# The low parts of 61 weight tiles: one subtraction on VectorE, or a copy on ScalarE and an accumulating DMA, in one layer of a hybrid backbone

## The chip, the cores and the metric

The kernel runs on one core of a Trainium2 chip. The metric is the device time of one execution in microseconds (us), lower is better; the profile gives beside it the span, which leaves out a little at both ends. The engines are PE (TensorE, matmuls; its weight loads are shown apart as PEld), DVE (VectorE), ACT (ScalarE), POOL (GpSimd) and SP (SyncE, which issues almost all DMAs). Each engine runs its instructions in a fixed order and waits on semaphores.

## The reference

One layer over 512 latent tokens and 256 context tokens of width 1024. What matters here is which weights are multiplied with what:

```python
h = rms_norm(x, g_norm1) * (1.0 + sc1) + sh1            # sc1, sh1, ... = silu(c) @ w_ada + b_ada
hc = rms_norm(ctx, g_norm1) * (1.0 + csc1) + csh1
aq, ak, av, dq, dk, dv, dz, da, db, ga, gd = split_cols(h @ w_in)
...
y_attn = window_ctx_attention(q_a, k_a, v_a, k_ac, v_ac, attn_sink)
o_dc, s_cf, s_cb = bidir_delta(...)                     # context scan, its states go on
o_dl, _, _ = bidir_delta(..., s_cf, s_cb)               # latent scan, chunks of 64
...
```

Each of the two mixers' results is projected to width 1024, weighted by a sigmoid gate, the two are summed and projected by `w_out`; a gated residual, a second norm and an MLP with squared ReLU (1024 to 4096 to 1024) follow.

## The kernel before, in words

**Split matmuls.** Nearly all matmuls run on fp32r operands, and to keep fp32 accuracy each operand is split into a high part (the value rounded to fp32r) and a low part (the value less its high part). A product is then three matmuls: high by high, high by low, low by high (`mm3`, L270, L271, L272; in the gate tiles and the branch projections the same three stand in L940 and L985). A weight tile holds 128 output columns and all rows of the contraction: 128x1024 numbers (512 KB), or 128x512 (256 KB) for a branch projection.

**Loading a weight tile** is `wload` (L254 to L263). SP starts the DMA of the raw tile into a slot of the ring `wr` (L256), which has NWR = 4 slots; ACT writes the high part `wh` (L261); DVE subtracts it from the raw tile and writes the low part `wl` (L262). The pairs `wh`, `wl` have NWS = 2 slots each. The list `wq` (L351 to L355) holds the tiles in the order in which PE takes them: 20 of `w_in` (the last three of DeltaNet's keys, attention's keys, queries and values, DeltaNet's values and queries, three gates), 8 of the first branch projection, 17 gates of `w_in`, 8 of the second branch projection, 8 of the output projection, 61 in all. `wnext` (L358) hands out the next one and starts to load the one behind it, so that one tile is ahead of the one in use. Two early tiles (L316) and the 64 tiles of the MLP (L1309, L1344, L1365) go through `wload` too, but into buffers of their own. The ring `wr` also takes the 32 tiles `wa` of the conditioning weights that are needed late; DVE multiplies them with the condition and sums along the row (`late_mod`, L1005, run in groups by `run_late` while the scan goes on, and the last eight beside the first quarter of the MLP).

**The stages**, by the span of the profile before:
- 0 to 66 us: norm and modulation of the inputs (`modulate`, L275 on DVE, L276 on ACT, L277 on DVE), with the two early tiles multiplied as each of the eight row blocks is ready.
- 66 to 320: key, query and value tiles; the attention and the inversion of the chunks' triangular matrices (a long sequence of small DVE operations, L770 and L771) are woven between them. Queries and keys pass a rotary embedding (`rope`: L405 is a multiplication on POOL, L404, L406 and L407 are on DVE).
- 320 to 520: the scan over chunks (`chain_step`), small dependent matmuls and DVE operations, with the branch projection of attention and the gate tiles as filler on PE.
- 520 to 606: the remaining gates, then the branch projection of DeltaNet (eight tiles of 12 matmuls of 512 columns), the output projection (eight tiles of 24), and the second norm.
- 606 to 957: the MLP, in quarters: eight tiles of the first matrix, eight of the second.

The order on each engine is fixed when the kernel is built: the code is woven by hand (`weave`), and a scheduler orders the instructions by their dependencies and the slots of the rings.

Of the kernel before, what the change touches and what calls it, by code (L numbers as in the profile page):

```python
# [11 lines left out]
AF = mybir.ActivationFunctionType  # L12
ALU = mybir.AluOpType
# [1 line left out]
PSUM = bass.MemoryType.PSUM  # L15

NU = 167
NWR, NWS = 4, 2
FILL = 144, 28, 36, (8, 7, 3)
INV = 2, 12, 18, 0  # L20
QTS = 7, 5, 4, 7, 3, 6, 10, 7
# [14 lines left out]
KT = D // P  # L36
# [60 lines left out]
def tile_layer(ctx: ExitStack, tc: tile.TileContext, I: dict, out: bass.AP, dbg=None):  # L97
    nc = tc.nc
    V, A, G, PE = nc.vector, nc.scalar, nc.gpsimd, nc.tensor
# [8 lines left out]
    def nm(s):  # L108
        uid[0] += 1
        return f"{s}_{uid[0]}"  # L110
# [19 lines left out]
    r32 = lambda ap: ap.bitcast(F32R)  # L130
# [120 lines left out]
        b.free()  # L251


    def wload(src, n=KT, bufs=None):  # L254
        raw = sb.tile([P, KT, P], F32, tag="wr", bufs=NWR, name=nm("wr"))[:, :n]
        nc.sync.dma_start(out=raw, in_=src)  # L256
        if bufs:
            hi, lo = (b.ap.rearrange("p (k c) -> p k c", k=KT) for b in bufs)
        else:
            hi, lo = (sb.tile([P, KT, P], F32, tag=t, bufs=NWS, name=nm(t))[:, :n] for t in ("wh", "wl"))  # L260
        A.activation(r32(hi), raw, AF.Copy)  # L261
        V.tensor_tensor(r32(lo), raw, hi, op=ALU.subtract)  # L262
        return r32(hi), r32(lo)  # L263

    def mm3(acc, w, xs, start=True, stop=True, ks=None):
# [20 lines left out]
    for kt in range(KT):  # L286
# [26 lines left out]
        if kt in EARLY:  # L313
            bb = alloc(1024), alloc(1024)
            ebufs += bb
            early.append((wload(I["win"][EARLY[kt]], bufs=bb), bank(2)))  # L316
# [28 lines left out]
    for n in range(2):  # L345
# [5 lines left out]
    wq = [(I["win"][t], KT) for t in (T_DK + 1, T_DK + 2, T_DK + 3, T_AK, *range(T_AQ, T_AQ + 4), T_AV, *range(T_DV, T_DV + 4),  # L351
                                      *range(T_DQ, T_DQ + 4), *(t + i for t, i in gates[:ND1]))]
    wq += [(I["wbr"][0, ct], 4) for ct in range(8)] + [(I["win"][t + i], KT) for t, i in gates[ND1:]]
    wq += [(I["wbr"][1, ct], 4) for ct in range(8)] + [(I["wout"][ct], KT) for ct in range(8)]
    wq = [lambda a=a: wload(*a) for a in wq]  # L355
    wn = [wq.pop(0)()]

    def wnext():  # L358
        w = wn.pop()
        if wq:  # L360
            wn.append(wq.pop(0)())
        return w

    def in_tile_steps(ti, with_ctx):

        for (_, e), t in zip(early, EARLY.values()):
            if t == ti:
                return e
        w = wnext()
        acc = bank(2 if with_ctx else 1)  # L370
        for k in range(KT):
            mm3(acc[:, :512], w, hx[k:k + 1], start=(k == 0), stop=(k == KT - 1), ks=[k])
            if with_ctx:
                mm3(acc[:, 512:768], w, hc[k:k + 1], start=(k == 0), stop=(k == KT - 1), ks=[k])
            if k < KT - 1:
                yield
        return acc
# [555 lines left out]
    def gate_tiles(todo):  # L933

        for kind, i in todo:
            w = wnext()
            acc = bank()
            for k in range(KT):
                for p, (x, y) in enumerate(((0, 0), (0, 1), (1, 0))):
                    PE.matmul(acc.ap, w[x][:, k, :], hx[k][y], start=(k == p == 0), stop=(k == KT - 1 and p == 2))  # L940
                    yield
            if kind == T_GA:
                g = alloc(SEQ)
                act(g.ap, acc.ap, AF.Tanh, scale=0.5)
                V.scalar_tensor_tensor(gat[i].ap, g.ap, 1.0, gat[i].ap, op0=ALU.add, op1=ALU.mult)
                g.free()
            else:
                t = alloc(SEQ, True)
                if kind == T_GD:
                    act(t.ap, acc.ap, AF.Tanh, scale=0.5)  # L950
                else:
                    silu2(t.ap, acc.ap)
                (gdt if kind == T_GD else szt).append(t)
            acc.free()
# [22 lines left out]
    def br_a():  # L977

        for ct in range(8):
            gat.append(alloc(SEQ, True))  # L980
            w = wnext()
            pa = bank()
            for j in range(4):
                for p, (x, y) in enumerate(((0, 0), (0, 1), (1, 0))):
                    PE.matmul(pa.ap, w[x][:, j, :], r32(Q[y][:, :, j, :]), start=(j == p == 0), stop=(j == 3 and p == 2))  # L985
                    yield
            A.activation(gat[ct].ap, pa.ap, AF.Copy)
            pa.free()
        for b in Qb:
            b.free()  # L990
# [8 lines left out]
    def late_mod(grp):  # L999

        for j in range(8):
            wa = sb.tile([P, KT, P], F32, tag="wr", bufs=NWR, name=nm("wa")).rearrange("p k c -> p (k c)")
            nc.sync.dma_start(out=wa, in_=I["wada2"][grp, j])
            t = alloc(1024)
            V.scalar_tensor_tensor(t.ap, wa, 0.5, scr.ap, op0=ALU.mult, op1=ALU.mult, accum_out=modT[:, grp, j:j + 1])  # L1005
            t.free()
            if j == 7:
                V.tensor_tensor(modT[:, grp], modT[:, grp], bada[:, 16 + 8 * grp:24 + 8 * grp], op=ALU.add)
            yield

    late = (x for grp in range(4) for x in late_mod(grp))
# [155 lines left out]
    for g in range(2):  # L1167
# [12 lines left out]
        for a in range(2):  # L1180
            lo, hi = quad(a, 0), quad(a, 1)
# [37 lines left out]
    for qq in range(2):  # L1219
# [3 lines left out]
        for a in range(2):  # L1223
            n = 2 * qq + a
# [16 lines left out]
    for ct in range(8):  # L1241
        w = wnext()
# [32 lines left out]
    for ct in range(8 - NHALF):  # L1275
        w = wnext()
# [29 lines left out]
    def load_first():  # L1306
        for i in range(NHALF):
            bufs = [alloc(1024), alloc(1024)]
            first.append([bufs, wload(I["wm1"][i], bufs=bufs)])  # L1309
# [27 lines left out]
    for hf in range(4):  # L1337
        act_ = []
        for f in range(FT):
            if first:  # L1340
                bufs, _, acc = first.pop(0)
            else:
                bufs = [alloc(1024), alloc(1024)]
                w = wload(I["wm1"][hf * FT + f], bufs=bufs)  # L1344
# [17 lines left out]
        for ct in range(8):  # L1362
            acc = bank()
            bufs = [alloc(1024), alloc(1024)]
            w = wload(I["wm2"][ct * 4 + hf], bufs=bufs)  # L1365
# [120 lines left out]
```

## Time and profile before

| | us |
|---|---|
| time, median of 3 runs (lowest to highest) | 960.3 (957.15 to 960.33) |
| the profiled execution | 959.2 |
| its span | 957.4 |
| PE busy | 917.7 |
| DVE busy | 597.9 |
| ACT busy | 449.3 |
| POOL busy | 36.4 |

The profiled execution is 1.8 us longer than its span, and 1.1 us under the median. In the views, L12 is line 12 of the kernel before; "out<-in" are the tiles that an instruction writes and reads; "<-" behind an idle time names what ended it ("issue": nothing that the profile shows). Matmuls are pipelined, so that one may count as busy while the next has begun.

### The profile page before, as it was taken

What the parts mean: (1) busy time and instruction counts of PE and PEld (TensorE: products, weight loads), DVE (VectorE), ACT (ScalarE), POOL (GpSimd) and SP (SyncE); (2) the same over time, 40 slices, a digit from 0 to 9 for tenths busy, and PEclk for the clock granted to TensorE, in tenths of its full rate; (3) what the DMA queues carried; (4) which work ended last, traced back from release to release, by engine and by line L of the source; (5) the groups of instructions that cost most, each with busy time, mean ns of one, the idle gap of its engine ahead of it and who ended that gap; (6) DMA issues with size and microseconds to landing.
All of it is one profiled execution on the core that took longest, in us unless ns stands there. A gap on an engine that the chain in (4) does not pass through costs nothing. (4 is left out here: it accounts for less than half of the span.)

```text
span 957.4 us, 18072 instructions
## 1 busy us (share of the span) xinstructions
PE 917.7 (96%) x7684; PEld 737.1 (77%) x7684; DVE 597.9 (62%) x1010; ACT 449.3 (47%) x827; POOL 36.4 (4%) x45
## 2 busy tenths in 40 slices
PE   7999989989999999869999999999999999999998
PEld 3578767876877677658887889988888888888886
DVE  0876688997788899745567665982365225423511
ACT  6456745337667887337555433561154115313400
POOL 0000221000000000100011000000000000000000
PEclk9999999999999999888999999999999999999999
DMA  9742012110000133850114544382164214322101
GB/s 354 250 167 67 23 47 66 48 64 24 12 21 25 38 107 111 295 192 25 46 61 129 185 134 154 119 272 72 35 212 134 82 66 130 113 66 71 62 33 55
DMA packets 29889, 99.77 MB, mean 104 GB/s; under 512 B 3696, under 2 KB 4208, under 8 KB 29808
## 3 DMA queue, kind: packets, MB, share of 16 engines
q1 hardware_dynamic: 29808, 98.62, 31.4%
q8 instruction: 60, 0.98, 0.4%
q14 instruction: 21, 0.17, 0.1%
HBM read 96.51 MB, written 2.10 MB: 103 GB/s over the span
## 5 line engine op out<-in xcount | busy, mean ns | idle before, releaser
L271 PE MATMUL banks<-m,m 128*128 128x512 f32 (+1 forms) x568 | 213.4, 378 | 0.0
L272 PE MATMUL banks<-m,m 128*128 128x512 f32 (+1 forms) x568 | 212.5, 377 | 0.0
L270 PE MATMUL banks<-m,m 128*128 128x512 f32 (+1 forms) x568 | 210.5, 379 | 1.7 <-ACT m L276 1.7
L261 ACT ACTIVATE m<-wr 128x1024 fp32r<-128x1024 f32 x66 | 69.9, 1059 | 150.3 <-PE banks L271 78.1
L270 PEld LDWEIGHTS banks<-m,m 128*128 128x128 f32 x568 | 105.5, 188 | 23.7 <-issue 1.9
L271 PEld LDWEIGHTS banks<-m,m 128*128 128x128 f32 x568 | 106.3, 188 | 21.3 <-DVE m L198 0.9
L272 PEld LDWEIGHTS banks<-m,m 128*128 128x128 f32 x568 | 106.4, 188 | 19.9
L262 DVE TENSOR_TENSOR m<-wr,m 128x1024 fp32r<-128x1024 f32 x66 | 80.6, 1224 | 63.9 <-PE banks L271 34.2
L270 PE MATMUL banks<-m,wh 128*128 128x512 f32 (+1 forms) x328 | 119.7, 365 | 0.0
L271 PE MATMUL banks<-m,wh 128*128 128x512 f32 (+1 forms) x328 | 116.4, 355 | 0.0
L272 PE MATMUL banks<-m,wl 128*128 128x512 f32 (+1 forms) x328 | 116.1, 355 | 0.1
L940 PE MATMUL banks<-m,wh 128*128 128x512 f32 x320 | 108.1, 413 | 0.0
L1367 DVE SCALAR_TENSOR_TENSOR m<-banks,modT,m 128x512 f32<-128x512 f32 x32 | 24.0, 750 | 104.0 <-PE banks L272 104.0
L261 ACT ACTIVATE wh<-wr 128x1024 fp32r<-128x1024 f32 (+1 forms) x61 | 57.7, 946 | 54.2 <-PE banks L940 24.4
L262 DVE TENSOR_TENSOR wl<-wr,wh 128x1024 fp32r<-128x1024 f32 (+1 forms) x61 | 65.8, 1079 | 20.8 <-ACT wh L261 20.7
L940 PEld LDWEIGHTS banks<-m,wh 128*128 128x128 f32 x320 | 62.1, 197 | 17.1 <-issue 4.1
L940 PE MATMUL banks<-m,wl 128*128 128x512 f32 x160 | 66.9, 418 | 4.3 <-issue 4.3
L272 PEld LDWEIGHTS banks<-m,wl 128*128 128x128 f32 x328 | 61.8, 189 | 9.3 <-DVE wl L262 0.6
L270 PEld LDWEIGHTS banks<-m,wh 128*128 128x128 f32 x328 | 61.9, 189 | 8.9 <-ACT m L276 0.4
L271 PEld LDWEIGHTS banks<-m,wh 128*128 128x128 f32 x328 | 62.0, 189 | 8.4 <-issue 0.5
L181 ACT ACTIVATE m<-m 128x512 fp32r<-128x512 f32 (+1 forms) x56 | 35.0, 630 | 47.4 <-DVE m L1350 19.8
L182 DVE TENSOR_TENSOR m<-m,m 128x512 fp32r<-128x512 f32 (+1 forms) x56 | 38.2, 689 | 20.9 <-ACT m L181 20.4
(232 smaller groups left out, 1325.8 us busy)
## 6 DMA issues: line engine op xcount, KB each, us to landing
wr<-in_wm SPq DMA_DIRECT2D x64, 512.0 KB, 3.5
wr<-in_win SPq DMA_DIRECT2D x39, 512.0 KB, 3.6
wa<-in_wada SPq DMA_DIRECT2D x32, 512.0 KB, 4.3
m<-in_wada SPq DMA_DIRECT2D x16, 512.0 KB, 10.1
m<-in_xT SPq DMA_DIRECT2D x8, 512.0 KB, 6.7
wr<-in_wbr SPq DMA_DIRECT2D x16, 256.0 KB, 2.7
wr<-in_wout SPq DMA_DIRECT2D x8, 512.0 KB, 3.6
out<-m SPq DMA_DIRECT2D x8, 256.0 KB, 2.0
```

Source lines behind the costliest of these rows:

```text
L181: A.activation(r32(hi), src, AF.Copy)
L182: (eng or V).tensor_tensor(r32(lo), src, hi, op=ALU.subtract)
L261: A.activation(r32(hi), raw, AF.Copy)
L262: V.tensor_tensor(r32(lo), raw, hi, op=ALU.subtract)
L270: PE.matmul(acc, w[0][:, k, :], xhi, start=(start and i == 0), stop=False)
L271: PE.matmul(acc, w[0][:, k, :], xlo, start=False, stop=False)
L272: PE.matmul(acc, w[1][:, k, :], xhi, start=False, stop=(stop and i == n - 1))
L940: PE.matmul(acc.ap, w[x][:, k, :], hx[k][y], start=(k == p == 0), stop=(k == KT - 1 and p == 2))
L1367: V.scalar_tensor_tensor(xn_[ct], acc.ap, modT[:, 3, ct:ct + 1], xn_[ct], op0=ALU.mult, op1=ALU.add)
```

## The change

For the 61 tiles of `wq`, DVE's subtraction is replaced by two steps: ACT writes the negative high part into the low part's buffer (it rounds the raw tile a second time, with a scale of -1), and a DMA that GpSimd issues reads the same weights from memory once more and adds them to what stands there. The early tiles and the MLP keep the subtraction. The ring of raw tiles has two slots and no longer four, the pairs have three and no longer two, and `wnext` keeps two tiles ahead.

```diff
-NWR, NWS = 4, 2
+NWR, NWS = 2, 3
+WAHEAD = 2
...
-    def wload(src, n=KT, bufs=None):
+    def wload(src, n=KT, bufs=None, late=False):
...
         A.activation(r32(hi), raw, AF.Copy)
-        V.tensor_tensor(r32(lo), raw, hi, op=ALU.subtract)
+        if late:
+            A.activation(r32(lo), raw, AF.Copy, scale=-1.0)
+            G.dma_start(out=r32(lo), in_=src, accum_op=ALU.add)
+        else:
+            V.tensor_tensor(r32(lo), raw, hi, op=ALU.subtract)
...
-    wq = [lambda a=a: wload(*a) for a in wq]
-    wn = [wq.pop(0)()]
+    wq = [lambda a=a: wload(*a, late=True) for a in wq]
+    wn = [wq.pop(0)() for _ in range(WAHEAD)]
...
-        w = wn.pop()
+        w = wn.pop(0)
```

In the changed kernel the lines behind the diff's first part move: the raw load is L258, the high part L263, ACT's negative part L265, the DMA L266, the subtraction L268, and what stood from L270 on stands six lines lower (L276 to L278 are `mm3`'s three matmuls).

On each engine 61 instructions move: DVE has 61 fewer, ACT 61 more, POOL issues 61 DMAs where it issued none. Each copies the whole tile: 45 of 512 KB and 16 of 256 KB, 27.3 MB of further reads of memory.

The first place is PE at the end of the input stage. `wh` and `wl` are the first tile of `wq`, numbers such as m_152 and m_153 are the modulated latent and context tokens, the other names are the two early tiles. Before, in the midst of the last row block:

```order
L271 MATMUL banks<-m_152,m_237 128x512
L272 MATMUL banks<-m_152,m_238 128x512
L271 MATMUL banks<-m_153,m_237 128x256
L272 MATMUL banks<-m_153,m_238 128x256
L272 MATMUL banks<-m_152,wl_469 128x512 [waits DVE_49]
L272 MATMUL banks<-m_153,wl_469 128x256
L270 MATMUL banks<-m_152,wh_468 128x512
L271 MATMUL banks<-m_152,wh_468 128x512
L272 MATMUL banks<-m_152,wl_469 128x512
L270 MATMUL banks<-m_153,wh_468 128x256
L271 MATMUL banks<-m_153,wh_468 128x256
L272 MATMUL banks<-m_153,wl_469 128x256
```

In the changed kernel, at the same row block:

```order
L277 MATMUL banks<-m_152,m_169 128x512 [waits DVE_49]
L278 MATMUL banks<-m_152,m_170 128x512
L277 MATMUL banks<-m_153,m_169 128x256 [waits DVE_49]
L278 MATMUL banks<-m_153,m_170 128x256
L277 MATMUL banks<-m_152,m_237 128x512
L278 MATMUL banks<-m_152,m_238 128x512
L277 MATMUL banks<-m_153,m_237 128x256
L278 MATMUL banks<-m_153,m_238 128x256
L278 MATMUL banks<-m_152,wl_469 128x512 [waits DMASW0_49]
L278 MATMUL banks<-m_153,wl_469 128x256
L276 MATMUL banks<-m_152,wh_468 128x512
L277 MATMUL banks<-m_152,wh_468 128x512
```

The matmuls with the first `wl`, which stood between the groups of the two early tiles, stand behind all of these groups, and the first of them waits for a DMA of POOL's queue (DMASW; DMAHW are SP's) in place of DVE.

The second place is ACT in the branch projection of DeltaNet: a high part for a coming tile alternates with the high part of a finished gated sum (`split`, L181 before). Before:

```order
L261 ACTIVATE wh_5877<-wr_5875 128x512 [waits DMAHW6_49,PE_49,Activation_49]
L181 ACTIVATE m_5824<-m_2935 128x512 [waits DVE_49]
L261 ACTIVATE wh_5899<-wr_5897 128x512 [waits DMAHW7_49,PE_49,Activation_49]
L181 ACTIVATE m_5825<-m_2967 128x512 [waits DVE_49]
L261 ACTIVATE wh_5921<-wr_5919 128x512 [waits DMAHW1_49,PE_49,Activation_49]
L181 ACTIVATE m_5826<-m_5599 128x512 [waits DVE_49]
```

In the changed kernel:

```order
L263 ACTIVATE wh_5932<-wr_5930 128x512 [waits DMAHW0_49,PE_49,Activation_49]
L265 ACTIVATE wl_5933<-wr_5930 128x512 [waits DMASW6_49,PE_49]
L182 ACTIVATE m_5877<-m_2962 128x512 [waits DVE_49]
L263 ACTIVATE wh_5955<-wr_5953 128x512 [waits DMAHW2_49,PE_49,Activation_49]
L265 ACTIVATE wl_5956<-wr_5953 128x512 [waits DMASW7_49,PE_49]
L182 ACTIVATE m_5878<-m_2995 128x512 [waits DVE_49]
L263 ACTIVATE wh_5978<-wr_5976 128x512 [waits DMAHW4_49,PE_49,Activation_49]
L265 ACTIVATE wl_5979<-wr_5976 128x512 [waits DMASW0_49,PE_49]
L182 ACTIVATE m_5879<-m_5648 128x512 [waits DVE_49]
```

Each high part is followed by the negative part of the same tile, and the finished sum's part stands behind both. In both kernels the high part waits for PE, which must be through with the slot's last tile.

The third place is POOL between 100 and 170 us of the span, where it computes parts of the chunks' matrices (L711) and the rotary embedding (L405). Before:

```order
L711 TENSOR_TENSOR m_1411<-c_nmask,btok 128x512 [waits DVE_49,Activation_49]
L405 TENSOR_TENSOR m_1055<-m_1055,m_454 128x512 [waits DVE_49,Activation_49,Pool_49]
L711 TENSOR_TENSOR m_1429<-c_nmask,btok 128x512 [waits PE_49]
L405 TENSOR_TENSOR m_1255<-m_1255,m_454 128x512 [waits DMAHW4_49,DVE_49,Activation_49]
L405 TENSOR_TENSOR m_1455<-m_1455,m_454 128x512 [waits DVE_49,Activation_49,Pool_49]
L405 TENSOR_TENSOR m_1524<-m_1524,m_454 128x512 [waits DVE_49,Activation_49]
```

In the changed kernel:

```order
L717 TENSOR_TENSOR m_1426<-c_nmask,btok 128x512 [waits DVE_49,Activation_49]
L266 DMA wl_1214<-in_win 128x1024 [waits DMASW4_49,PE_49,Activation_49]
L411 TENSOR_TENSOR m_1068<-m_1068,m_454 128x512 [waits DVE_49,Pool_49]
L717 TENSOR_TENSOR m_1444<-c_nmask,btok 128x512 [waits PE_49]
L266 DMA wl_1415<-in_win 128x1024 [waits DMASW5_49,PE_49,Activation_49]
L411 TENSOR_TENSOR m_1269<-m_1269,m_454 128x512 [waits DMAHW4_49,DVE_49]
L266 DMA wl_1500<-in_win 128x1024 [waits DMASW6_49,PE_49,Activation_49]
L411 TENSOR_TENSOR m_1470<-m_1470,m_454 128x512 [waits DVE_49,Pool_49]
L266 DMA wl_1558<-in_win 128x1024 [waits DMASW7_49,Activation_49]
L411 TENSOR_TENSOR m_1540<-m_1540,m_454 128x512 [waits DVE_49,Activation_49]
```

The DMAs stand between these operations, and each waits for ACT's negative part and for an earlier DMA of the queue, most of them for PE too; what stands behind one on POOL waits with it.

## The prediction

> **What bounds the kernel now.** I read the page's busy times first, and with them its list of DMA issues (KB each, median us from issue to landing), which the new work will be measured by.
>
> ```profile
> PE 917.7 (96%) x7684; PEld 737.1 (77%) x7684; DVE 597.9 (62%) x1010; ACT 449.3 (47%) x827; POOL 36.4 (4%) x45
> ...
> wr<-in_win SPq DMA_DIRECT2D x39, 512.0 KB, 3.6
> wa<-in_wada SPq DMA_DIRECT2D x32, 512.0 KB, 4.3
> ...
> wr<-in_wbr SPq DMA_DIRECT2D x16, 256.0 KB, 2.7
> wr<-in_wout SPq DMA_DIRECT2D x8, 512.0 KB, 3.6
> ```
>
> PE is busy for 96% of the span. Taking 65.8 us of work off DVE cannot take 65.8 us off the time: it is worth only what PE loses to DVE. So the next view is the waits of PE.
>
> ```profile
> PE banks L699 <- issue: 6.5, 3, 4.0
> PE banks L221 <- DMA m<-in_wada: 6.0, 1, 6.0
> PE banks L800 <- issue: 4.4, 3, 2.1
> PE banks L940 <- issue: 4.3, 1, 4.3
> PE banks L699 <- DVE m L729: 2.7, 1, 2.7
> PE banks L487 <- DVE m L577: 2.4, 1, 2.4
> PE banks L395 <- ACT m L392: 2.2, 2, 1.8
> PE banks L270 <- ACT m L276: 1.7, 2, 1.3
> PE banks L823 <- DVE m L583: 1.1, 1, 1.1
> PE banks L791 <- DVE m L781: 1.0, 1, 1.0
> PE banks L1063 <- DVE m L1056: 0.9, 1, 0.9
> ```
>
> The columns are the total in us, how often, and the longest. 15.2 us (L699, L800, L940) are put down to "issue", which no DVE work explains, and 6.0 us to the first DMA. DVE itself makes 2.7 + 2.4 + 1.1 + 1.0 + 0.9 = 8.1 us. Where in the span these lie is read from busy times by stage; the second group of rows is DVE's subtraction L262 alone.
>
> ```profile
> 105.00:320.00 215.00, 200.51 (x2030) 157.81 (x2016) 184.84 (x345) 126.46 (x243) 16.43 (x13) 0.98 0.12 38
> 320.00:520.00 200.00, 186.39 (x3093) 149.78 (x3094) 140.18 (x261) 118.93 (x295) 14.99 (x24) 0.95 0.37 118
> 520.00:560.00 40.00, 39.96 (x182) 32.42 (x182) 29.76 (x44) 17.98 (x28) 0.00 (x0) 1.00 0.49 154
> ```
>
> ```profile
> 105.00:320.00 215.00, 19.64 (x17) 0.98 0.12 38
> 320.00:520.00 200.00, 23.61 (x22) 0.95 0.37 118
> ```
>
> The columns after the stretch and its length are the busy times of PE, PEld, DVE, ACT and POOL, the granted clock, the DMA share and GB/s. From 105 to 320 DVE is busy for 184.84 of 215 us, 86%, and 19.64 of that is L262: this is the stage in which DVE can hold PE up. From 520 to 560 PE is full (39.96 of 40), and anything that makes a weight late there shows in the time at once.
>
> **The change part by part.** *DVE's relief.* The groups of the work that goes and of the work that is like the new one on ACT:
>
> ```profile
> L261 ACT ACTIVATE wh<-wr 128x1024 fp32r<-128x1024 f32 (+1 forms) x61 | 57.7, 946 | 54.2 <-PE banks L940 24.4
> L262 DVE TENSOR_TENSOR wl<-wr,wh 128x1024 fp32r<-128x1024 f32 (+1 forms) x61 | 65.8, 1079 | 20.8 <-ACT wh L261 20.7
> ```
>
> 61 subtractions of 1079 ns go. Of the 8.1 us of waits for DVE I take two thirds as recovered, since a chain gets shorter only by the subtractions that stood in it: 5.4 us. Matmuls count as busy while they overlap, so that short waits are hidden in a busy PE, and one stretch of that stage, with DVE full, had a lower clock:
>
> ```profile
> 135.00:140.00 5.00, 4.50 (x230) 2.98 (x232) 5.00 (x6) 1.49 (x3) 0.00 (x0) 0.66 0.22 64
> ```
>
> At 0.66 these 5 us hold at most 5 x 0.34 = 1.7 us of lost clock. For both I take 2 us. The relief is -7.4. Its bounds are 0 (other work fills the chains) and -19.6 (DVE bounds the whole stage from 105 to 320, and all of its L262 comes off); I stay near the waits because they are what PE was seen to lose.
>
> *ACT's second pass.* 61 passes like L261: 57.7 us, from 449.3 to 507.0, 53% of the span. Most of it lies beside other work. PE's waits for ACT (L395 2.2, L270 1.7) grow with ACT's load, by 57.7/449.3 = 13%, some 0.5; a chain step that finds a pass of 1.06 ahead of it a few times makes it 1. Bounds: 0 and 3. Where the cover is gone, from 300 to 320 (19.05 of 20 us busy, below), a pass costs its full length.
>
> ```profile
> 300.00:320.00 20.00, 17.79 (x102) 13.56 (x99) 17.74 (x34) 19.05 (x39) 0.00 (x0) 1.00 0.09 27
> ```
>
> *The way to the low part gets longer.* It was ACT's pass and DVE's pass. It becomes: ACT's pass, ACT's second pass, the issue on POOL, the DMA. A slot comes free when PE is through with a tile, and its new content is needed two tiles later, so the way has the time of two tiles. How long a tile takes shows ACT's high parts, which wait for PE's end of a tile:
>
> ```profile
> 537.23 0.63 ACT L261 ACTIVATE wh<-wr 128x512 fp32r<-128x512 f32 x1 [0.33 <-PE banks L271]
> 539.38 0.63 ACT L181 ACTIVATE m<-m 128x512 fp32r<-128x512 f32 x1 [1.52 <-DVE m L1248]
> 540.02 0.63 ACT L261 ACTIVATE wh<-wr 128x512 fp32r<-128x512 f32 x1
> ```
>
> ```profile
> 567.68 1.06 ACT L261 ACTIVATE wh<-wr 128x1024 fp32r<-128x1024 f32 x1 [3.89 <-PE banks L271]
> 568.65 0.63 ACT L1270 ACTIVATE m<-m 128x512 f32<-128x512 f32 x1
> 573.18 1.06 ACT L261 ACTIVATE wh<-wr 128x1024 fp32r<-128x1024 f32 x1 [3.89 <-PE banks L271]
> ```
>
> A branch tile takes 540.02 - 537.23 = 2.8 us, an output tile 573.18 - 567.68 = 5.5. No accumulating DMA and no DMA of POOL stands in the trace. Its lower bound is the plain load of the same bytes, 2.7 us for 256 KB and 3.6 for 512 KB; as the upper one I take twice that, 5.4 and 7.2, since it reads two operands. I take it nearer to the lower end, 3.4 and 5.1, adding only the part that grows with size: the rows differ by 0.9 us per 256 KB, so some 0.7 and 1.5. POOL's issue I take as 0.7, between 0 and 2.1 (its longest operation beside DVE, below), and 0.3 for the handing over.
>
> Small tiles: 0.63 + 0.63 + 0.3 + 0.7 + 3.4 = 5.7 against 2 x 2.8 = 5.6 us of cover. With three slots the period is (5.7 + 2.8)/3 = 2.83, so 8 x 0.03 = 0.2 us are lost. At the upper ends (5.4 and 2.1) the way is 9.1, the period 3.95, the loss 9.2. The first output tile is worse off: its 512 KB take 1.06 + 1.06 + 0.3 + 0.7 + 5.1 = 8.2 us, and the cover ahead of it is still two branch tiles, 5.6: 2.6 us late, once. From there on the cover is 11 us, and nothing is lost below a way of 11. Together +2.8. At the lower ends (3.6, no issue time) the way is 6.0 and the loss 0.4; at the upper ones (7.2 and 2.1) it is 11.7, the first output tile 6.1 late and the seven behind it 0.2 each, with the branch tiles 17. In the first branch projection and the gates up to 520 the scan's matmuls lie between the tiles' own, and the cover is longer.
>
> By the Trainium skill (DMA: Bandwidth & Descriptors, Anatomy of one DMA — SWDGE path) such a DMA takes about 2.0 us and the bytes at 436 GB/s, an estimate of 2.6 and 3.2 us, and by it the first output tile would come 0.7 us late, 1.9 less than I take, and the sum would be -4.0. No row of this trace shows such a DMA.
>
> The Trainium skill speaks against the change in Collectives: The Full Stack, The bandwidth ceiling: an add in a DMA engine runs at half the rate because it reads two sources. The nearest row, the plain load's 3.6 us, would make the sum 1.5 us lower than the doubled part does; I side with the dearer one.
>
> *The input stage.* PE has lost the first tile's low matmuls as filler for the wait on the last row block:
>
> ```profile
> 61.13 0.61 PE L272 MATMUL banks<-m,wl 128*128 128x512 f32 x2
> 61.58 0.40 PE L270 MATMUL banks<-m,wh 128*128 128x512 f32 x1
> ...
> 62.63 0.88 PE L270 MATMUL banks<-m,m 128*128 128x512 f32 x4
> ```
>
> 1.5 us of them (61.13 to 62.63) go behind the wait. Against this DVE's subtraction at 59.85 (1.22 us) no longer stands ahead of the last block's own operations, so the wait ends about 1.2 sooner. The new DMA has to be in by then; if it is late PE has no other work. I take +1, bounds -1 and +4.
>
> *The raw ring of two slots.* Late conditioning tiles and the MLP's first quarter share it. A slot turns over in 4.3 us of load and DVE's pass of 1.23 (row below), 5.5 us; one 5.5-us MLP tile beside it just fits. I take +0.5, bounds 0 and 6.
>
> ```profile
> L1005 DVE SCALAR_TENSOR_TENSOR m<-wa,m 128x1024 f32<-128x1024 f32 x32 | 38.8, 1229 | 11.4 <-DMA wa<-in_wada 11.4
> ```
>
> *POOL.* Rotary multiplications stand behind DMAs that wait for PE. They ran beside a stretched DVE operation already:
>
> ```profile
> L405 POOL TENSOR_TENSOR m<-m,m x5: 1707/1747/2097, 109.8 to 165.7; 128x512 f32<-128x512 f32 x5
> ```
>
> The waits are for tiles that PE has long left, so nothing, or 1 us if one comes late.
>
> The sum: -7.4 + 1 + 2.8 + 1 + 0.5 = -2.1. The profiled execution of 959.2 would become 957.1; the median of the runs stands 1.1 higher, so 958.2.
>
> **The rivals.** *The DMA is the bound (slower).* If issue and accumulating DMA together take more than 11 - 1.06 - 1.06 - 0.3 = 8.6 us for 512 KB, the gates and output tiles wait at every turn. At 10 us the way is 12.4: (12.4 + 5.5)/3 - 5.5 = 0.5 us for each of 8 output tiles, 4; for the branch tiles, at half of it, the way is 6.6, the period 3.13 and the loss 2.6; the first output tile comes 6.8 late; the gates before 520 lose perhaps 0.2 each, 3. That is 16.4 in place of 2.8, so +11.5 and 972; at 12 us, by the same steps with 0.3 for each gate, it nears 984. For it: no row shows such a DMA, and PE is full there. Against: 4.3 us is the longest median of any 512 KB tile that is loaded beside the running work.
>
> *DVE bounds more than PE's waits show (faster).* If it sets the pace of the stage from 105 to 320, two thirds of its 19.6 us come off there, 13, in place of 5.4, and some 3 in the scan: 958.2 - 10.6 = 948. For it: 86% busy. Against: PE is busy for 200.51 of 215 us there.
>
> *The two raw slots hold the scan up (slower).* Two conditioning tiles in flight allow one each 5.5/2 = 2.8 us; DVE waited 11.4 us for them with four slots. If that doubles and half of it reaches PE, between 376 and 430 where the scan's matrices are combined, the time is 958.2 + 5.7 = 964.
>
> **How the numbers follow.** About 0.5%, 4.8 us, is what a measurement of this kernel can tell from no change. The forecast's case has 0.48: with its own range of 951 to 966 I give 0.17 of it to faster by over 0.5%, 0.24 to within, 0.07 to slower. The slow DMA has 0.20 (0.19 slower, 0.01 within); DVE as the bound 0.20 (0.18 faster, 0.02 within); the raw ring 0.12 (0.08 slower, 0.04 within). That makes 0.35 faster, 0.31 within, 0.34 slower. The range goes from 944, which leaves out the far end of the DVE case (0.07), to 982, which leaves out the far end of the slow DMA (0.10).
>
> **What would show it.** In the profile after, DVE's busy time should be near 532 and ACT's near 507; PE's waits for L699, L487, L791 and L823 on DVE should shrink to about a third. A DMA row for `wl` with a median of 4 to 6 us from issue to landing for 512 KB bears the forecast out; over 8.6 the first rival holds. PE's waits should name a DMA at the first output tile (some 2.6 us) and at the first key tile near 64 us. The forecast is wrong if PE waits for `wl` at tile after tile, or if the stage from 105 to 320 shrinks by over 10 us.

## The result, and the profile after

The changed kernel takes 1004.5 us in the median (999.38 to 1011.01) against 960.1 us before: a ratio of 1.0473, 95% interval [1.0407, 1.054]. It is slower by 44 us where 958.2, no change, was forecast. Its profiled execution took 1006.3 us and has a span of 1004.5 us. All times and ratios below are of runs in the faster of two states that executions show; two of the four runs of late_old_rings fell in the slower one and are left out.

The changed kernel's page, busy times and DMA rows:

```profile
PE 932.5 (93%) x7684; PEld 746.2 (74%) x7684; DVE 545.5 (54%) x949; ACT 498.6 (50%) x888; POOL 87.6 (9%) x106
...
q1 hardware_dynamic: 29808, 98.62, 30.0%
q0 software_dynamic: 8784, 27.79, 16.2%
...
wr<-in_win SPq DMA_DIRECT2D x39, 512.0 KB, 3.9
wl<-in_win POOLq DMA_DIRECT2D x37, 512.0 KB, 8.0
...
wl<-in_wbr POOLq DMA_DIRECT2D x16, 256.0 KB, 5.2
wr<-in_wout SPq DMA_DIRECT2D x8, 512.0 KB, 5.1
```

DVE's busy time fell by 52.4 us and ACT's rose by 49.3, less than the 65.8 and 57.7 that the prediction took from the rows of the groups: the rows add up to more than the page's busy time, where instructions overlap (639.8 us for DVE before, against 597.9). POOL's queue moved 27.79 MB, which is 45 x 512 KB and 16 x 256 KB; the 27.3 MB given with the change is a slip. The accumulating DMA takes 8.0 us in the median from the start of its issue to landing for 512 KB of `w_in` and 5.2 for 256 KB, and the plain load of an output tile beside it takes 5.1 where it took 3.6. The changed kernel's waits of PE:

```profile
PE banks L705 <- issue: 12.9, 4, 4.5
PE banks L278 <- DMA wl<-in_wout: 11.3, 3, 6.6
PE banks L806 <- ACT m L799: 8.7, 2, 4.7
...
PE banks L278 <- DMA wl<-in_wbr: 5.1, 2, 3.7
PE banks L946 <- DMA wl<-in_win: 5.1, 2, 4.9
PE banks L1228 <- DVE m L1223: 3.5, 1, 3.5
PE banks L705 <- DVE m L735: 3.2, 2, 2.7
PE banks L278 <- DMA wl<-in_win: 2.5, 1, 2.5
```

24.0 us are waits for `wl` by name (11.3 + 5.1 + 5.1 + 2.5), which is half of the loss. The page's busy times say what kind the rest is: PE's idle time (span less busy) grew from 39.7 to 72.0 us, by 32.3, and PE was busy for 14.8 us more with the same 7684 matmuls; together this is the 47.1 us by which the span grew. Most of the 14.8 shows in the stretches that follow waits for `wl`. The changed kernel, five such waits each with the stretch behind it (the columns as in the prediction; the clock is the third from the end):

```profile
60.00:66.00 6.00, 3.75 (x20) 2.88 (x18) 4.09 (x8) 4.31 (x6) 1.11 (x2) 1.00 0.92 212
66.00:72.00 6.00, 5.15 (x21) 4.46 (x22) 1.96 (x3) 5.88 (x8) 0.00 (x0) 0.72 0.65 132
...
452.00:458.00 6.00, 1.38 (x6) 0.77 (x5) 1.40 (x3) 5.92 (x21) 0.38 (x1) 0.89 0.96 213
458.00:464.00 6.00, 5.75 (x69) 4.87 (x70) 2.50 (x7) 0.57 (x3) 0.00 (x0) 0.54 0.52 150
564.00:569.00 5.00, 1.25 (x6) 0.74 (x5) 2.61 (x4) 1.78 (x3) 0.99 (x2) 1.00 1.01 261
569.00:575.00 6.00, 6.00 (x20) 4.72 (x20) 1.38 (x2) 1.78 (x3) 0.86 (x1) 0.72 0.86 252
588.00:592.00 4.00, 0.89 (x5) 0.42 (x4) 2.65 (x4) 2.52 (x3) 1.45 (x2) 1.00 0.89 214
592.00:600.00 8.00, 8.00 (x28) 6.40 (x29) 0.75 (x1) 1.34 (x2) 0.00 (x0) 0.79 0.84 204
629.00:637.00 8.00, 1.42 (x9) 1.22 (x10) 3.61 (x5) 2.73 (x4) 0.88 (x1) 0.82 0.90 246
637.00:645.00 8.00, 8.00 (x54) 8.00 (x54) 1.82 (x4) 0.83 (x2) 0.00 (x0) 0.75 0.21 70
```

Behind each wait PE runs at 0.54 to 0.79 for 6 to 8 us: 6 x 0.28 + 6 x 0.46 + 6 x 0.28 + 8 x 0.21 + 8 x 0.25 = 9.8 us more. (The kernel before has no such wait near 66 us, and its clock is 1.00 from 60 to 105.) The DMA share in the waits is 0.89 to 1.01: while PE waits, the DMA engines are full.

Where the time went, by stage. The boundaries are the first or last start of a PE line (half products, branch projection, scan, gates, the norm's sum), so that the same work is compared; us, from the profiled executions of the kernels that are compared by stage. One stage of one execution can differ by some 2 us without a cause in it: the change and late_to_gates treat the first 45 tiles alike, and their input stages take 109.8 and 107.3.

| kernel | input | attention | combining | scan | gates | branch, output | MLP | span |
|---|---|---|---|---|---|---|---|---|
| before | 104.8 | 211.3 | 114.8 | 73.3 | 30.1 | 65.4 | 357.7 | 957.4 |
| the change | 109.8 | 210.9 | 120.9 | 82.6 | 34.4 | 87.5 | 358.4 | 1004.5 |
| rings_only | 105.7 | 212.8 | 117.5 | 72.9 | 29.8 | 63.3 | 358.7 | 960.7 |
| no_dma | 104.9 | 209.5 | 113.6 | 72.7 | 30.4 | 63.3 | 358.8 | 953.2 |
| plain_dma | 105.7 | 209.7 | 115.6 | 78.1 | 30.1 | 73.0 | 359.4 | 971.6 |
| unread | 113.1 | 210.0 | 120.3 | 78.6 | 30.1 | 80.8 | 358.2 | 991.1 |
| mods_apart | 108.8 | 213.7 | 127.5 | 73.6 | 29.7 | 82.2 | 359.8 | 995.3 |
| halves | 106.2 | 210.1 | 119.3 | 77.8 | 33.5 | 77.9 | 358.0 | 982.8 |
| late_scan | 105.7 | 212.9 | 118.8 | 82.0 | 34.3 | 63.9 | 357.9 | 975.5 |
| late_to_gates | 107.3 | 211.9 | 121.2 | 83.2 | 35.1 | 63.3 | 357.9 | 979.9 |
| late_from_branch | 105.3 | 212.5 | 117.7 | 72.9 | 29.2 | 83.0 | 358.0 | 978.6 |
| traffic_four | 105.2 | 211.5 | 114.6 | 72.9 | 30.1 | 75.2 | 361.6 | 971.1 |
| pass_only | 104.4 | 212.9 | 114.7 | 73.5 | 29.3 | 64.8 | 361.7 | 961.3 |

The change loses 22.1 us from the branch projection to the norm, 9.3 in the scan, 6.1 in the combining, 5.0 in the input stage and 4.3 in the gates. In the attention stage, for which DVE's relief was counted on, it wins 0.4.

### The profile page after: what moved, and what is told of

Read it like the earlier page. It is cut to its first block, busy times and chain, and to the rows that moved or that the text cites. A ratio compares the mean times of both kernels' runs of the same rounds, so it can differ in the third digit from the quotient of the medians.

```text
span 1004.5 us, 18150 instructions
## 1 busy us (share of the span) xinstructions
PE 932.5 (93%) x7684; PEld 746.2 (74%) x7684; DVE 545.5 (54%) x949; ACT 498.6 (50%) x888; POOL 87.6 (9%) x106
## 3 DMA queue, kind: packets, MB, share of 16 engines
q1 hardware_dynamic: 29808, 98.62, 30.0%
q0 software_dynamic: 8784, 27.79, 16.2%
## 4 chain that ended last, share of the span: by engine, by line
PE 71%; issue 10%; DMA 7%; ACT 6%; DVE 4%; POOL 1%; SPq 0%; POOLq 0%; DVEq 0%; ACTq 0%
PE banks L276 16%; PE banks L277 16%; PE banks L278 15%; PE banks L946 6%; DMA wl<-in_win 2%; PE banks L991 2%; DMA wa<-in_wada 2%; PE banks L222 2%; PE banks L1057 2%; DMA wl<-in_wout 1%; PE banks L534 1%; PE banks L705 1%; ACT m L146 1%; PE banks L1088 1%; PE banks L1069 1%
## 5 line engine op out<-in xcount | busy, mean ns | idle before, releaser
L278 PE MATMUL banks<-m,m 128*128 128x512 f32 (+1 forms) x568 | 212.5, 377 | 0.0
L276 PE MATMUL banks<-m,m 128*128 128x512 f32 (+1 forms) x568 | 210.7, 379 | 1.2 <-ACT m L282 1.2
L263 ACT ACTIVATE m<-wr 128x1024 fp32r<-128x1024 f32 x66 | 69.9, 1060 | 154.5 <-PE banks L277 58.5
L278 PE MATMUL banks<-m,wl 128*128 128x512 f32 (+1 forms) x328 | 119.1, 365 | 19.0 <-DMA wl<-in_wout 11.3
L268 DVE TENSOR_TENSOR m<-wr,m 128x1024 fp32r<-128x1024 f32 x66 | 80.8, 1225 | 85.7 <-ACT m L263 52.3
L276 PEld LDWEIGHTS banks<-m,m 128*128 128x128 f32 x568 | 105.5, 188 | 23.7 <-ACT m L282 2.5
L276 PE MATMUL banks<-m,wh 128*128 128x512 f32 (+1 forms) x328 | 122.0, 372 | 0.4 <-DVE m L1274 0.4
L278 PEld LDWEIGHTS banks<-m,m 128*128 128x128 f32 x568 | 106.3, 188 | 19.5
L277 PE MATMUL banks<-m,wh 128*128 128x512 f32 (+1 forms) x328 | 119.6, 365 | 0.2 <-issue 0.2
L263 ACT ACTIVATE wh<-wr 128x1024 fp32r<-128x1024 f32 (+1 forms) x61 | 57.7, 945 | 60.8 <-PE banks L277 24.6
L278 PEld LDWEIGHTS banks<-m,wl 128*128 128x128 f32 x328 | 64.0, 196 | 29.9 <-DMA wl<-in_wout 12.1
L276 PEld LDWEIGHTS banks<-m,wh 128*128 128x128 f32 x328 | 64.4, 196 | 9.9 <-issue 0.7
L946 PEld LDWEIGHTS banks<-m,wh 128*128 128x128 f32 x320 | 61.5, 195 | 13.0
L277 PEld LDWEIGHTS banks<-m,wh 128*128 128x128 f32 x328 | 64.2, 196 | 8.9 <-issue 0.9
L265 ACT ACTIVATE wl<-wr 128x1024 fp32r<-128x1024 f32 (+1 forms) x61 | 57.2, 937 | 0.1
L1011 DVE SCALAR_TENSOR_TENSOR m<-wa,m 128x1024 f32<-128x1024 f32 x32 | 39.2, 1231 | 30.8 <-DMA wa<-in_wada 30.5
L266 POOL DMA_DIRECT2D wl<-in_win x37 | 32.2, 870 | 272.2 <-ACT wl L265 222.1
```

The costliest lines, as they stand in the source:

```text
L265: A.activation(r32(lo), raw, AF.Copy, scale=-1.0)
L266: G.dma_start(out=r32(lo), in_=src, accum_op=ALU.add)
L276: PE.matmul(acc, w[0][:, k, :], xhi, start=(start and i == 0), stop=False)
L277: PE.matmul(acc, w[0][:, k, :], xlo, start=False, stop=False)
L278: PE.matmul(acc, w[1][:, k, :], xhi, start=False, stop=(stop and i == n - 1))
```

## The experiments

All times are medians; the ratio is to the kernel before on the same chip, with its 95% interval.

**The rings alone (rings_only).**

```diff
-    wq = [lambda a=a: wload(*a, late=True) for a in wq]
+    wq = [lambda a=a: wload(*a) for a in wq]
```

> The three rings of the change (two raw slots, three pairs, two tiles ahead), but DVE subtracts for every tile as before. Theory A (the two raw slots, shared with the late conditioning tiles, cost the stage in which the scan's matrices are combined, some 15 us; the accumulating DMA costs the stage from 520 on and the input stage, some 28 us): about 15 us of the 44 stay, 972 to 978, DVE waits over 25 us for the conditioning tiles, and PE is full from 520 to 600 as before. Theory B (only the longer way to the low part matters, the raw ring does nothing): 958 to 962. Theory C (the rings alone cause all of it): about 1000.

961.2 us, 1.005 [1.0024, 1.0076]: the three rings cost 4.4 us and not 15 (961.2 - 956.8, the time of before on that chip). DVE waits longer for the conditioning tiles, as its row shows, here of the run with the rings alone:

```profile
DVE m L1011 <- DMA wa<-in_wada: 18.4, 16, 2.8
```

It was 11.4 us before and 30.5 in the change. Two raw slots are a small part of the loss by themselves.

**The DMA taken out (no_dma).**

```diff
-            G.dma_start(out=r32(lo), in_=src, accum_op=ALU.add)
```

> The change without its DMA: the low part is left as the negative high part, so the sum that the DMA makes is left out. Theory A: PE's waits for the low parts after 520 and in the input stage go (28 us), the raw ring's 15 us stay and DVE's relief remains: 968 to 975. If instead the traffic of the second reads slows the code fetches and the conditioning tiles too (theory D), the stage from 380 to 460 comes back as well: 952 to 960.

956.6 us, 0.9997 [0.9973, 1.0021]. All that the change loses hangs on the DMA: without it the time is that of before, to a quarter of a per cent. Against the rings alone, on the same chip, DVE's relief and ACT's second pass win 961.2 - 956.6 = 4.6 us together, and the rings take that back. That is all that the change wins apart from its DMA, and it is no more than other places in the arena can make (rings_hole, below), so that it is not shown to be DVE's relief alone.

**The rings of before (late_old_rings).**

```diff
-NWR, NWS = 2, 3
-WAHEAD = 2
+NWR, NWS = 4, 2
+WAHEAD = 1
```

> The negative part on ACT and the accumulating DMA, but the rings of before: four raw slots, two pairs, one tile ahead. Theory A: the cover of the way falls from two tiles to one (5.5 us for a tile of 512 KB), while the way is 1.06 + 1.06 + 0.3 + 8 = 10.4 us, so each tile that PE takes without other work between loses 3 to 5 us: 24 tiles after 520 lose some 90 us, and the time is 1040 to 1120; DVE's waits for conditioning tiles fall back to 11 us. Theory C (the rings cause all of it): 955 to 965.

1051.9 us, 1.0991 [1.0904, 1.1078], from 1046.4 and 1057.3. With one tile of cover in place of two the same DMA costs some 95 us: the second tile ahead, with the third pair that it needs, is what keeps the change from losing twice as much.

**The conditioning tiles apart (mods_apart).**

```diff
-            wa = sb.tile([P, KT, P], F32, tag="wr", bufs=NWR, name=nm("wa")).rearrange("p k c -> p (k c)")
+            wab = alloc(1024)
+            wa = wab.ap
...
             t.free()
+            wab.free()
```

> The change, with the late conditioning tiles in buffers of their own from the arena, so that the two raw slots serve the weights alone. Theory A: the 15 us of the stage from 380 to 460 come back, and so may the 6.7 us at the last output tile, whose raw tile no longer shares; 980 to 992. Theory B (the raw ring does nothing): 1000 to 1008.

997.3 us, 1.0427 [1.0375, 1.0479], between the two expectations. By stage the scan and the gates come back whole (73.6 and 29.7 us), the branch and output stage by 5.3 us, and the combining gets 6.6 us longer: the conditioning tiles now take buffers of the arena (the part of the on-chip memory that `alloc` gives out to the tiles of the other work), and PE waits longer for ACT's copy there, 14.8 us for 8.7 (why is not shown):

```profile
PE banks L806 <- ACT m L799: 14.8, 2, 8.9
```

The chain of events in the scan of the changed kernel shows why the raw slots mattered there; SP, ACT, POOL in turn:

```profile
443.67 1.47 SPq L258 DMA_DIRECT2D wr<-in_win  x2
```

```profile
447.27 1.04 ACT L263 ACTIVATE wh<-wr 128x1024 fp32r<-128x1024 f32 x1
448.21 1.04 ACT L265 ACTIVATE wl<-wr 128x1024 fp32r<-128x1024 f32 x1
```

```profile
449.55 0.86 POOL L266 DMA_DIRECT2D wl<-in_win  x1 [5.16 <-ACT wl L265]
```

The raw gate tile is loaded at 443.67, after three conditioning tiles have used the slots; its DMA is issued at 449.55 and lands 8.7 us later, and PE stands from 453.4 to 458.25 (the row of 452 to 458 above).

**A plain copy in place of the addition (plain_dma).**

```diff
-            G.dma_start(out=r32(lo), in_=src, accum_op=ALU.add)
+            G.dma_start(out=r32(lo), in_=src)
```

> The change with the same DMA of GpSimd, but without the adding: the low part becomes a copy of the weights, so the sum is left out. Theory E (the adding makes the DMA slow: 8.0 us for 512 KB and 5.2 for 256 KB, against 3.6 and 2.7 of a plain load): the DMA lands in 3.6 to 4.8 and 2.7 to 3.6 us, and the time is 957 to 968. Theory F (GpSimd's queue is slow whatever it does): 7 to 8 us and 5 us, and 995 to 1005.

972.7 us, 1.0154 [1.0125, 1.0183]. Its page:

```profile
q0 software_dynamic: 8784, 27.79, 8.2%
...
wl<-in_win POOLq DMA_DIRECT2D x37, 512.0 KB, 4.8
...
wl<-in_wbr POOLq DMA_DIRECT2D x16, 256.0 KB, 3.9
```

The time lies above theory E's range and far below theory F's: GpSimd's plain DMA costs 16.1 us over no DMA at all (972.7 - 956.6), and the addition the other 30 or so (1.0473 against 1.0154 of before, from two sets of runs). The queue rows show what the addition costs the DMA engines. The same 27.79 MB hold the 16 engines for 8.2% of 971.6 = 80 us without the addition and for 16.2% of 1004.5 = 163 us with it, 2.04 times as long. The Trainium skill has that rule, for ReduceScatter, in Collectives: The Full Stack, The bandwidth ceiling (an add reads two sources and runs at half the rate), and the two rows agree with it. An output tile needs 0.52 MB of plain load, 1.6 us of all engines by the 301 us for 98.62 MB of the queue of SP, and 3.1 us of adding: 4.7 of the 5.5 us that PE takes for it.

**PE does not read the low part (unread).**

```diff
-        return r32(hi), r32(lo)
+        return r32(hi), r32(hi if late else lo)
```

> The change with every pass and every DMA, but PE takes the high part where it took the low part, so that it never waits for the DMA; the low part's products are left out. Theory G (PE's waiting for the DMA is the loss): 955 to 965. Theory D (the second reads slow the other loads, and through them the scan): much of the loss between 376 and 460 and in the input stage stays, 970 to 985.

996.4 us, 1.0396 [1.0344, 1.0447]: neither expectation. The run does not tell the two apart as it was meant to. With nobody waiting for the low part, ACT's negative pass of the next tile stands ahead of that tile's high part and waits for its raw load, which the DMAs in flight slow down. The waits of ACT in this run:

```profile
ACT wl L265 <- DMA wr<-in_win: 27.9, 14, 4.6
ACT wl L265 <- DMA wr<-in_wout: 26.9, 8, 6.1
```

And those of PE, in which no `wl` stands any more:

```profile
PE banks L276 <- ACT wh L263: 5.4, 2, 3.8
PE banks L276 <- ACT m L182: 5.0, 2, 3.2
```

A raw output tile lands in 5.9 us here, and the branch and output stage takes 80.8 us, 17.5 more than with the rings alone. So the DMAs hold PE up even when PE takes nothing from them, through the high part. As ACT's order changed too, the run does not show that traffic alone does it.

**Two DMAs for each tile (halves).**

```diff
-            G.dma_start(out=r32(lo), in_=src, accum_op=ALU.add)
+            for hh in range(2):
+                kk = slice(hh * (n // 2), (hh + 1) * (n // 2))
+                G.dma_start(out=r32(lo[:, kk]), in_=src[:, kk], accum_op=ALU.add)
```

> Each accumulating DMA is issued as two, each for half of the tile's rows of the contraction, so that PE can begin with the first half. If the time of the DMA grows with its bytes (8.0 - 5.2 = 2.8 us per 256 KB), the first half of a 512 KB tile is there 2.8 us sooner, the second one some 0.9 us later, and most of PE's waits after 520 shrink by 2 to 3 us each: 985 to 997. If the time is a fixed latency, nothing is won: 1003 to 1012.

989.2 us, 1.0318 [1.0278, 1.0357], in the range that was expected if the time grows with the bytes: 15 us come back, 9.6 of them from the branch projection to the norm. PE's waits for output tiles are 5.7 us in place of 11.3, though each half takes longer than a branch tile of the same size took in the change:

```profile
wl<-in_win POOLq DMA_DIRECT2D x74, 256.0 KB, 6.4
...
wl<-in_wout POOLq DMA_DIRECT2D x16, 256.0 KB, 6.5
```

**One part of the tiles, or the other (late_to_gates, late_from_branch).**

```diff
-    wq = [lambda a=a: wload(*a, late=True) for a in wq]
+    wq = [lambda a=a, n=n: wload(*a, late=n < 45) for n, a in enumerate(wq)]
```

> The changed rings, and the accumulating DMA for the first 45 tiles (keys to gates); the second branch projection and the output projection, 16 tiles, are subtracted by DVE as before. The stage from the last gate to the second norm was 22.1 us longer in the change. Theory A: that comes back, 977 to 986. If the losses hang together (theory D: traffic of the whole kernel), it stays above 990.

982.2 us, 1.0247 [1.021, 1.0284].

> The counterpart of the run that kept the accumulating DMA for the first 45 tiles: here only the last 16 (second branch projection, output projection) have it, the first 45 are subtracted by DVE, with the rings of the change. If the losses of the two parts simply add, 44 = 25 + x - 4.4 (the rings count in both), so x is 24, and the time is 978 to 984. If the losses come from the traffic of the whole kernel, clearly less, below 972.

With `n >= 45` in place of `n < 45`: 982.2 us, 1.0286 [1.0242, 1.033]. The parts add up: 25.2 + 25.4 - 4.4 for the rings, which both hold, is 46, and the change lost 44. Against the rings alone each loses in the stages of its own tiles (the table), and no further loss needs both.

**Traffic without waiting (traffic_only, traffic_four, pass_only).** The last 16 tiles get their subtraction on DVE; the negative pass and the DMA go into 2, then 4, buffers of the arena that nobody reads, so that what they add up is thrown away; the control has the passes alone.

```diff
+        if late == 2:
...
+            V.tensor_tensor(r32(lo), raw, hi, op=ALU.subtract)
+            A.activation(r32(j), raw, AF.Copy, scale=-1.0)
+            G.dma_start(out=r32(j), in_=src, accum_op=ALU.add)
...
```

> As the run before, with the same 16 negative parts and accumulating DMAs at the same places, but into two buffers that nobody reads, while DVE subtracts the low part that PE takes; what is added is thrown away. Theory G (PE's wait for the low part itself is the loss): 960 to 966, since the way to the low part is short again. Theory H (the DMA engines are full there: the second reads delay the loads of the raw tiles): 972 to 984, and the raw output tiles land in over 5 us.

976.5 us, 1.0208 [1.0166, 1.0251]. ACT waited 13.5 us for the two buffers, so it was repeated with four.

> The run with 16 accumulating DMAs into buffers that nobody reads, with four such buffers in place of two, because ACT waited 13.5 us there for the DMA that still filled the buffer. If that wait was the 15 us over the run with the rings alone, the time falls to 960 to 965 (theory G: traffic costs nothing by itself). If the traffic delays the raw loads (theory H), 968 to 978, raw output tiles still land in over 5 us, and PE waits for ACT's high parts.

973.2 us, 1.0154 [1.0125, 1.0183].

> The same with ACT's 16 extra passes into the four unread buffers and no DMA: the control for the run before. Both theories: ACT's passes lie beside PE's work, 959 to 964; what the run before has over this one is the DMA alone.

966.8 us, 1.0094 [1.0071, 1.0118], above the expected 959 to 964; its profiled execution, of 961.3 us span, lies some 4 us under that. The rows of the run with four buffers (L272 is the negative pass, L182 the high part of a finished sum, L286 the first of `mm3`'s matmuls):

```profile
ACT m L272 <- DMA wr<-in_wout: 13.3, 6, 5.4
```

```profile
PE banks L286 <- ACT m L182: 4.4, 1, 4.4
```

```profile
wr<-in_wout SPq DMA_DIRECT2D x8, 512.0 KB, 6.2
```

The last of them in the control without the DMA:

```profile
wr<-in_wout SPq DMA_DIRECT2D x8, 512.0 KB, 3.4
```

In the branch and output stage the rings alone take 63.3 us, the passes 64.8, passes and traffic 75.2, and the real thing 83.0. So of the 19.7 us that the accumulating DMA and its passes cost there, about 10 are traffic that makes the raw tiles late (6.2 us to land, against 3.4 in the control), and about 8 PE's wait for the result. The split is rough. By the medians the traffic costs 973.2 - 966.8 = 6.4 us, not 10. And ACT's negative passes stand ahead of some high parts in the run with four buffers, which makes the traffic dearer than it is in the real thing: with the DMA in its place (late_from_branch) raw output tiles land in 4.3 us.

**The scan's stage by itself (late_scan, traffic_scan, pass_scan).** The same for tiles 21 to 45; the arena has room for one unread buffer there.

```diff
-    wq = [lambda a=a: wload(*a, late=True) for a in wq]
+    wq = [lambda a=a, n=n: wload(*a, late=20 <= n < 45) for n, a in enumerate(wq)]
```

> The rings of the change; the negative part on ACT and the accumulating DMA for tiles 21 to 45 alone (first branch projection and gates, the scan's stage), DVE's subtraction for the rest. If the loss of this stage (15 us) is made there, 961 + 10 to 17 = 971 to 978. If it is handed down from the input stage or the attention's tiles, 960 to 965.

975.8 us, 1.0205 [1.0172, 1.0239]: the loss of the scan (82.0) and of the gates (34.3) is made there. Its waits of PE:

```profile
PE banks L946 <- DMA wl<-in_win: 7.1, 2, 5.4
PE banks L1228 <- DVE m L1223: 3.1, 1, 3.1
```

> The same 25 passes and accumulating DMAs into one buffer that nobody reads (what they add up is thrown away), while DVE subtracts the low parts. Theory H (traffic: the conditioning tiles and raw tiles land later, and the scan waits for them): 968 to 976. Theory G (PE's wait for the low part): 960 to 965.

> The control: the same 25 passes of ACT into the unread buffer, no DMA. 960 to 965 by both theories; above that, ACT's passes themselves hold up the scan.

988.4 us, 1.0334 [1.0311, 1.0357], with the DMAs into the one buffer, and 954.0, 0.9965 [0.9947, 0.9983], without them; neither is in an expected range. The first is above the real thing, so it measures something else as well: with one buffer ACT waits for the last DMA before it can write again (13.6 us, the rows for `in_win` and `in_wbr`), with the scan's copies behind it. It shows only that traffic and a blocked ACT can cost more than the change does there; the split between waiting and traffic in this stage stays open.

**A buffer out of the arena (rings_hole, before_hole).** The control had come out below the kernel before, so the buffer was taken out alone. The edit, as it stands in the kernel before (before_hole):

```diff
...
+        if late:
+            alloc(1024)
         V.tensor_tensor(r32(lo), raw, hi, op=ALU.subtract)
...
-    wq = [lambda a=a: wload(*a) for a in wq]
+    wq = [lambda a=a, n=n: wload(*a, late=n == 22) for n, a in enumerate(wq)]
```

> The rings of the change, DVE's subtraction for all tiles, and one buffer of 4 KB per partition taken out of the arena when the 21st tile is loaded. If the other places that the arena then gives out are what shortened the combining stage in the control run, 952 to 956. If it was the idle passes of ACT, 959 to 963, as with the rings alone.

> The kernel before with one buffer taken out of the arena when the 23rd tile is loaded (at the 21st the arena is too full for it), nothing else. If the places in the arena are the cause, 950 to 955; if they only help where two raw slots are short, 955 to 960.

958.2 us, 0.9995 [0.998, 1.001], with the rings of the change and 960.5, 1.0015 [0.9996, 1.0035], with those of before; the first lies between its two expectations, the second just above its own. The places that the arena then gives out win back what the new rings cost (1.005 of before without them), and win nothing for the kernel before. None of the kernels beats the kernel before by the 0.5% that can be told.

## Why the prediction was wrong

**DVE's relief and ACT's pass: right in kind, a little small.** -7.4 + 1 = -6.4 was forecast, -4.6 measured (no_dma against rings_only, with the reservation made there). The waits for L487, L823 and L791 did go from the list; the one for L699 stayed, 3.2 us for 2.7. For POOL nothing was forecast, and DVE's wait for the rotary multiplication is 3.6 us in both kernels.

**The raw ring: mis-sized.** +0.5 was taken, with a bound of 6; +4.4 was measured, for the three rings together. This is close to the rival of the two raw slots (5.7); DVE's wait for the conditioning tiles grew from 11.4 to 18.4 us with the rings alone, not quite the double that the rival took.

**The way to the low part: the step that failed.** It said that an accumulating DMA of 512 KB takes 5.1 us and its issue 0.7, that two tiles of cover are then enough nearly everywhere, and +2.8. The DMA takes 8.0 us with its issue in place of 5.8, and 1.06 + 1.04 + 0.3 + 8.0 = 10.4 us stand against a cover of 5.6 at the first output tile. PE waited 3.1 us there, until 591.9, where 2.6 was foreseen: the place was right. So the size of the DMA alone is the smaller half of the mistake. At its own upper ends, 7.2 and 2.1, the step gave 17 us; the DMA with its issue stayed below that 9.3, and below the 8.6 us from which the first rival was to decide, and the loss came to some 46 us over no DMA (1.0473 against 0.9997 of before). Three things were not in the sum.

- A wait costs more than its length. Five waits brought 9.8 us of lower clock behind them. The 0.66 beside a DVE wait stood in the prediction's own rows, as a gain, and was not carried over to the losses. The Trainium skill says this in TensorE: Matmul & The Clock Gate, HAM oscillation (a gap of over 3.4 us drops the clock, and each such gap pays for it again). Here a wait of 2.5 us, shortly after one of 0.55, was enough.
- The addition takes from the others. The DMA was priced as a latency of its own. It holds the DMA engines for twice the time of a load, and the raw output tiles beside it land in 5.1 us in place of 3.6. That is a cost at which no wait for `wl` is named (traffic_four).
- "The scan's matmuls lie between the tiles' own, and the cover is longer" failed at the scan: there the two raw slots, with conditioning tiles in them, started the way late, so that the DMA's 8.7 us came on top (mods_apart brings the scan back, late_scan makes the loss alone).

The DMA's own time grows with the traffic, too. In a quiet stretch of the changed kernel, from 260 to 300 us with a DMA share of 0.21, two of 512 KB took 6.2 and 5.8 us, hardly more than the 5.8 that were taken with the issue. The two issued at 449.6 and 451.5, where the DMA engines are full, took 8.7 and 10.5, and the third branch tile, of 256 KB, took 7.9 (PE waits 3.7 us for it, the row of 564 to 569). The page before could have told: the loads of the inputs in the first 40 us, of 512 KB as well, took about two and three times the 3.6 us there, where the DMA engines are nearly full. These are two rows of the list that the prediction left out, and the page's DMA share in 40 slices of 24 us, in tenths, of which the first two are 9 and 7:

```profile
DMA  9742012110000133850114544382164214322101
...
m<-in_wada SPq DMA_DIRECT2D x16, 512.0 KB, 10.1
m<-in_xT SPq DMA_DIRECT2D x8, 512.0 KB, 6.7
```

**The input stage:** +1 with a bound of +4 was taken, and 5.0 measured in this execution (2.5 in late_to_gates, which treats these tiles alike): the wait for the first `wl` of 2.5 us was foreseen at its place, near 64 us, and the clock of 0.72 from 66 to 72 was not.

**The rivals.** The slow DMA was right in kind, given 0.20 and 972; its rule (a loss at every output tile above 8.6) was not what happened. Nor did the prediction's own signs of error show: 8.0 us lies between its 6 and its 8.6, PE waited for `wl` eight times and not at tile after tile, and the stage from 105 to 320 hardly shrank. Output tiles in the middle of the row run at 5.5 us, and most of the loss sits at the transitions: the first `wl`, the gate behind conditioning tiles, the third branch tile behind the gates, the change from branch to output tiles, and the last output tile. There the order on ACT added a wait of its own. ACT in the changed kernel, at that tile:

```profile
625.21 1.06 ACT L263 ACTIVATE m<-wr 128x1024 fp32r<-128x1024 f32 x1 [7.54 <-DMA wr<-in_wm]
626.18 1.05 ACT L263 ACTIVATE wh<-wr 128x1024 fp32r<-128x1024 f32 x1
627.13 0.62 ACT L1276 ACTIVATE m<-m 128x512 f32<-128x512 f32 x1
627.65 1.04 ACT L265 ACTIVATE wl<-wr 128x1024 fp32r<-128x1024 f32 x1
```

An MLP tile's pass stands ahead and waits 7.5 us for its load, and the last `wl` is issued behind it, at 629.65: PE waits until 636.6. DVE as the hidden bound is not borne out: with its work gone, and ACT's passes in its place, the attention stage is 1.8 us shorter (no_dma), not 13, and PE's waits for ACT, 3.4 us there before and 4.5 then, hide no such gain.

What stays open is the split of the scan's and the combining's loss between PE's wait and the traffic, and why "issue" before L705 grew from 6.5 to 12.9 us (to 10.2 with the rings alone).

## What to carry to other kernels

Before work is moved from an engine to a DMA, ask three prices and not one: its latency against the cover at each transition between stages, its share of the DMA engines beside what already runs there, and the lower clock behind each wait that it makes on TensorE. An engine that is 86% busy is not thereby the bound: here the stage got 1.8 us shorter when 20 us of its work went and ACT took over passes for it. A control that leaves out only the new operation (no_dma) gives what the change would be worth if that operation cost nothing; take it first.

## What the runs showed of the hardware that was not expected

- An accumulating DMA from memory takes 8.0 us for 512 KB and 5.2 for 256 KB in the median from issue to landing; a plain one of the same queue 4.8 and 3.9; the loads of SP's queue 3.6 and 2.7. The Trainium skill's fit for GpSimd's path (DMA: Bandwidth & Descriptors, Anatomy of one DMA — SWDGE path) gives an estimate of 3.2 and 2.6: the plain runs here lie 1.6 and 1.3 above it, beside other traffic.
- Cut in two, each half of a 512 KB tile takes 6.4 us, not 5.2; the second is issued about 1 us behind the first, so that both are in flight together.
- Issuing such a DMA holds GpSimd for 0.86 us, a plain one for 0.53 (plain_dma).
